# Sixteen-column products ahead of eight blocks left out, eleven warm-up products, and bias rows stored 32 times instead of 128

## The chip, the cores and the metric

The kernel is one launch on one core of a Trainium2 chip. The core has a matrix engine (TensorE, PE in the profile, with its weight loads shown apart as PEld), a vector engine (DVE), a scalar engine (ACT), GpSimd (POOL), a queue engine that issues transfers (SP), and 16 DMA engines which bring data from the chip's memory. Each engine works through its own list of instructions in order and waits on semaphores where it needs something from another. The metric is the device time of the launch in microseconds (us); lower is better.

## What is computed

One decoder layer on 256 tokens of width 2048, everything in float32:

```
h    = rms_norm(x, attn_norm_g);  q, k, v, p = split(h @ w_in)          # 2048 x 4096
q, k = rms_norm per head;         a = softmax(q k^T * scale + bias) v   # 8 heads of 128, causal
m    = (window mean of p over 2/4/8/16 tokens - p) @ pool_w * pool_scale
x    = x + concat(a, m) @ w_out
u    = rms_norm(x, ffn_norm_g) @ w_up                                   # 2048 x 11264
y    = conv_b + causal depthwise convolution (width 3) of u
x    = x + (silu(gate half of y) * value half of y) @ w_down            # 5632 x 2048
```

The bias of a head is a table of 32 learned values, looked up by the distance of query and key; a key after its query gets a very large negative number. With 256 tokens and blocks of 256 the block selection of the reference selects nothing, and plain causal attention is left.

## The kernel before

All weights are laid out on the host in the order of use, as chunks of 128 x 2048 floats (1 MB). A chunk is loaded by SP into one of four `raw` buffers (L111), then split in two: ACT writes `wh`, the weights rounded to the matrix engine's shorter float (L121), and DVE writes `wl`, what the rounding left (L122). The activations are split in the same way into a high and a low part. A product of weights and activations is then three short products: high by high, low by high, high by low; low by low is dropped. Three pairs `wh`, `wl` exist, so PE can be a chunk or so behind the split.

The program is a list `steps` of half chunks, written out by hand. Step `u` uses half `u` of the weights, and after it the functions hooked to that step are issued (`hooks`). Ahead of each even step stands the split of the chunk two further on. The order of the instructions on each engine is the order in which this loop issues them. The stages are:

- 16 steps for the values (`val_half`, L158), 32 steps in token layout for keys and queries (`tok_half`, L168). In between come the sums of squares of the input (L310, L290), the bias row of each head (`bias_rows`, L262) and, from step 35 on, the attention head by head (`scores` L361, `probs_T` L387, `head_out` L397 and L398), placed between the products of the steps.
- 16 steps for the pooling inputs, then 34 for the output projection and the pooling weights. From here on the blocks are in feature layout: `feat_block` makes 256 output features in one accumulator in two halves, from four steps (or three) of eight products each. One such product is a pair of instructions: `wh` against 512 moving columns (high and low part of the activations side by side, L175) and `wl` against 256 moving columns (the high part, L177). This pair is the unit of work of most of the run.
- The feed-forward part: the 22 groups of the inner width go in three thirds (`THIRDS`). A third runs a gate block and a value block for each of its groups, then eight `down` blocks, one for every 256 output features. The very last block uses `feat_sum` (L184), three instructions in place of a pair.

At the first gate block's end `stats2` computes the second norm: `row_scale` multiplies a matrix of ones by the squares in full float32 (L290), which PE does as two passes of 256 columns. These two are issued behind the gate block's last product and ahead of the first value block.

`feat_block` has a flag `lead`. Where it is set, a product of `wh` (128 columns, stationary) and 16 columns of `wl` goes into the accumulator ahead of the block's first product (L490); the first real product then starts that accumulator anew, so nothing of it remains in the result. The flag is set for eight blocks: the third block of the output projection (g == 2), the first gate block of each third, the first value block, and the first down block of each third.

At the very start PE multiplies `ones` by `ones` eight times in full float32 (L218), two passes each, while the first weights are on their way.

The bias: `bias_rows` computes one row of 384 numbers per head (`rsb`, on 8 partitions) and POOL stores it to memory 128 times per head (`band`, L264). `bias_tile` then reads for four heads a tile of 128 x 4 x 256 in which partition p starts one element further left than partition p - 1 (L270), and this shift makes the rows of the distances. The first tile is read at step 24, the second when the fourth head's scores are done. `T`, the tile, shares its buffer with the table `onehot` that `bias_rows` reads.

Of the kernel before, what the change touches and what calls it, by code (L numbers as in the profile page):

```python
# [23 lines left out]
F32 = mybir.dt.float32  # L24
# [5 lines left out]
P = 128  # L30
D = 2048
S = 256
NT = S // P
HD = 128
NH = 8
# [6 lines left out]
L = 384  # L42
CH = 2048
HALF = CH // 2
# [5 lines left out]
OK = (0, 4, 12, 8)  # L50
# [5 lines left out]
def down_order(blocks):  # L56

    a, b, *rest = blocks
    return a[:-1] + b[:-1] + a[-1:] + b[-1:] + [h for c in rest for h in c]
# [18 lines left out]
def layer(ctx: ExitStack, tc: tile.TileContext, xT, wts, par, relT, ident_d, onehot_d, icnt_d, out):  # L78
    nc = tc.nc
# [5 lines left out]
    dram = ctx.enter_context(tc.tile_pool(name="dram", bufs=1, space=bass.MemoryType.DRAM))  # L85
# [3 lines left out]
    def acc(name):  # L89
        return mm.tile([P, 2, 512], F32, name=name, tag="acc")  # L90
# [4 lines left out]
    def small(name):  # L95
        return sm.tile([P, 512], F32, name=name, tag="small")
# [7 lines left out]
    raws, wparts = {}, {}  # L104
# [82 lines left out]
    def feat_half(u, act, k0, ps, first, last, mm=feat_mm):  # L187
        wh, wl = half(u)
        for m in range(2):
            mm(ps[m], wh, wl, act,  # L190
               [(slice(k * 256 + m * P, k * 256 + (m + 1) * P), k0 + k) for k in range(4)],
               first, last)
# [21 lines left out]

    nc.vector.memset(ones, 1.0)
    ps = small("ps_start")
    for _ in range(8):
        nc.tensor.matmul(ps[:, :P], ones, ones, start=True, stop=True)  # L218
    def x_first():
        hi, lo = xh[:, 0, 0, :], xh[:, 0, 1, :]  # L220
# [24 lines left out]
    onehot = early.tile([32, 2 * S], F32, name="onehot", tag="T")  # L245
    rsb = early.tile([NH, L], F32, name="rsb", tag="e", bufs=3)
    icnt = early.tile([P, 4, S], F32, name="icnt")
    band = dram.tile([NH, P, L], F32, name="band")

    def load_consts():  # L250
        nc.sync.dma_start(pv, par)
# [7 lines left out]
    def bias_rows():  # L259
        nc.gpsimd.memset(rsb, NEG)  # L260
        ps = small("ps_rel")
        nc.tensor.matmul(ps[:NH, :S], onehot[:, S:S + NH], onehot[:, :S], start=True, stop=True)  # L262
        nc.vector.tensor_copy(rsb[:, :S], ps[:NH, :S])
        nc.gpsimd.dma_start(band, rsb[:, None, :].to_broadcast([NH, P, L]))  # L264

    def bias_tile(h0):
        t = early.tile([P, 4, S], F32, name="T", tag="T")
        src = bass.AP(tensor=band.tensor, offset=band.offset + h0 * P * L + P - 1,
                      ap=[[L - 1, P], [P * L, 4], [1, S]])
        nc.gpsimd.dma_start(t, src)  # L270
        return t


# [21 lines left out]
    st = {}  # L295
# [149 lines left out]
    def pool_half(u, g0):  # L445

        wh, wl = half(u)
        cat = st["cat"]
        for i in range(2):
            g = g0 - i  # L450
            ps = [(small if i else aux)("ps_pool")[:, :S] for m in range(2)]
            for m in range(2):
                feat_sum(ps[m], wh, wl, cat,
                         [(slice((2 * i + k) * 256 + m * P, (2 * i + k) * 256 + (m + 1) * P), 8 + 2 * g + k)
                          for k in range(2)], True, True)
            st["pool", i] = ps
        for i in range(2):
            g, ps = g0 - i, st.pop(("pool", i))
            parts = [(8 + 2 * g + m, ps[m], col(C_PS + 2 * g + m)) for m in range(2)]
            for k, src, gc in parts:  # L460
                nc.scalar.activation(cat[:, k, 0, :], src, AF.Copy, scale=gc)
            for k, src, gc in parts:
                nc.vector.scalar_tensor_tensor(cat[:, k, 1, :], src, gc, cat[:, k, 0, :].bitcast(F32),
                                               op0=OP.mult, op1=OP.subtract)


    steps, hooks, pre, deferred = [], [], {}, []
# [9 lines left out]
                    post(box["ps"])  # L477
            steps.append([run])

    def feat_block(act, ks, post, final=False, lead=False):  # L480
        box, runs = {}, []
        for i, k0 in enumerate(ks):
            def run(u, i=i, k0=k0):
                if i == 0:
                    box["acc"] = None if final else acc("ps_feat")
                    box["ps"] = [small("ps_feat")[:, :S] if final else box["acc"][:, m, :] for m in range(2)]
                    if lead:
                        wh, wl = wparts[u // 2]
                        o = (u % 2) * HALF
                        nc.tensor.matmul(box["ps"][0][:, :16], wh[:, o:o + P], wl[:, o:o + 16], start=True, stop=True)  # L490
                feat_half(u, act(), k0, box["ps"], i == 0, i == len(ks) - 1, feat_sum if final else feat_mm)
                if i == len(ks) - 1:
                    post(box["ps"] if final else box["acc"])
            runs.append([run])
        return runs
# [5 lines left out]
    XK = (0, 4, 8, 12)  # L501
# [39 lines left out]
    for b in range(2):  # L541
# [4 lines left out]
        for j in range(4):  # L546
            h, u = 4 * b + j, at + 2 * j
# [8 lines left out]
    late = {}  # L556
# [20 lines left out]
    def residual(ps, g):  # L577
        x2 = add_to_x2(ps, g)
        if g == 0:
            nc.scalar.activation(late["sq"], x2, AF.Square)  # L580
            return
        s = late["pool"].tile([P, 2, S], F32, name="xs", tag="y0", bufs=2)
        nc.scalar.activation(s, x2, AF.Square)
        nc.vector.tensor_tensor(late["sq"], late["sq"], s, op=OP.add)

    def x2_split(g):

        if "h" not in late:
            late["h"] = keep.tile([P, KT, 2, S], F32R, name="x2h", tag="h")
        x2, dst = late["x2"], late["h"]  # L590
        for k in range(2 * g, 2 * g + 2):
            nc.scalar.activation(dst[:, k, 0, :], x2[:, k, :], AF.Copy, scale=col(C_FFN + k))
        for k in range(2 * g, 2 * g + 2):
            nc.vector.scalar_tensor_tensor(dst[:, k, 1, :], x2[:, k, :], col(C_FFN + k),
                                           dst[:, k, 0, :].bitcast(F32), op0=OP.mult, op1=OP.subtract)

    def stats2():
        late["rrow"] = keep.tile([P, S], F32, name="rrow2", tag="rrow")
        row_scale(late["rrow"], late["sq"][:, 0, :], late["pool"])

    o0 = len(steps)
    outs = []
    for g in range(D // 256):
        def post(ps, g=g):
            residual(ps, g)
            if g == D // 256 - 1:
                sq = late["sq"]
                nc.vector.tensor_tensor(sq[:, 0, :], sq[:, 0, :], sq[:, 1, :], op=OP.add)
                x2_split(g)
        outs.append(feat_block(lambda: st["cat"], OK, post, lead=(g == 2)))  # L610
    pools = [[lambda u, g=g: pool_half(u, g)] for g in (3, 1)]
    steps += out_order(outs, pools)
    for g in range(D // 256 - 1):
# [25 lines left out]
    def gate(ps, g):  # L639
        if g == 0:  # L640
            stats2()
        conv_in(ps, 0)

        def rest():
            y = conv(2 * g, 0)
            nc.scalar.activation(y, y, AF.Silu)  # L646
            late["gate"] = y
        deferred.append(rest)

    def value(ps, g, j):  # L650
        conv_in(ps, 1)

        def rest():
            if j == 0:
                late["hid"] = keep.tile([P, KT, 2, S], F32R, name="hid", tag="c")
            y = conv(NF + 2 * g, 1)
            hid, ks = late["hid"], slice(2 * j, 2 * j + 2)
            nc.vector.tensor_tensor(y, y, late["gate"], op=OP.mult)  # L658
            nc.scalar.activation(hid[:, ks, 0, :], y, AF.Copy)  # L659
            nc.vector.tensor_tensor(hid[:, ks, 1, :], y, hid[:, ks, 0, :].bitcast(F32), op=OP.subtract)  # L660
        deferred.append(rest)

    def down(ps, g, last, final):
        x2 = late["x2"]
        if final:
            for m in range(2):
                k = 2 * g + m
                nc.vector.tensor_tensor(x2[:, k, :], ps[m], x2[:, k, :], op=OP.add)
                nc.sync.dma_start(out[:, k, :], x2[:, k, :])
            return  # L670
        add_to_x2(ps, g)
        if last:
            nc.sync.dma_start(out[:, 2 * g:2 * g + 2, :], x2[:, 2 * g:2 * g + 2, :])

    for n, (g0, g1) in enumerate(THIRDS):
        for g in range(g0, g1):
            steps += feat_block(lambda: late["h"], XK, lambda ps, g=g: gate(ps, g), lead=(g == g0))
            steps += feat_block(lambda: late["h"], XK, lambda ps, g=g, j=g - g0: value(ps, g, j), lead=(g == 0))
        blocks = []
        for g in range(D // 256):  # L680
            final = n == 2 and g == D // 256 - 1
            blocks.append(feat_block(lambda: late["hid"], range(0, 2 * (g1 - g0), 4),
                                     lambda ps, g=g, n=n, final=final: down(ps, g, n == 2, final), final,
                                     lead=(g == 0)))
        steps += down_order(blocks)

    for u, f in hooks:
# [1 line left out]
    n = len(steps)  # L689
# [76 lines left out]
```

## Time and profile before

| what | value |
|---|---|
| median of 3 runs | 1047.64 us (1046.87 to 1047.82) |
| the profiled execution | 1047.67 us, of which the profile's span is 1045.9 us |
| matrix engine busy | 1039.5 us, 5794 products and 5794 weight loads |
| vector engine, scalar engine busy | 702.7 us, 509.5 us |
| transfers | 200.42 MB, 192 GB/s over the span |

The profile is of one execution. A line such as L175 is the line of the code that issued the instruction, and `ps_feat<-x2h,wh` says which tile it writes and which it reads. "Busy" of PE means that products were under way. Matmuls are pipelined: the next one starts before the one ahead has ended. So the distance from start to start is what one product costs, and its printed duration is longer than that. A product of full float32 is two instructions.

### The profile page before, as it was taken

What the parts mean: (1) busy time and instruction counts of PE and PEld (TensorE: products, weight loads), DVE (VectorE), ACT (ScalarE), POOL (GpSimd) and SP (SyncE); (2) the same over time, 40 slices, a digit from 0 to 9 for tenths busy, and PEclk for the clock granted to TensorE, in tenths of its full rate; (3) what the DMA queues carried; (4) which work ended last, traced back from release to release, by engine and by line L of the source; (5) the groups of instructions that cost most, each with busy time, mean ns of one, the idle gap of its engine ahead of it and who ended that gap; (6) DMA issues with size and microseconds to landing.
All of it is one profiled execution on the core that took longest, in us unless ns stands there. A gap on an engine that the chain in (4) does not pass through costs nothing.

```text
span 1045.9 us, 13805 instructions
## 1 busy us (share of the span) xinstructions
PE 1039.5 (99%) x5794; PEld 897.7 (86%) x5794; DVE 702.7 (67%) x756; ACT 509.5 (49%) x531; POOL 3.7 (0%) x13
## 2 busy tenths in 40 slices
PE   9999999999999999999999999999999999999998
PEld 7887888898888888888888888888888888888887
DVE  6654768967677777776554677777755557777753
ACT  7533555555455545554334454554543445455431
POOL 0000000000000000000000000000000000000000
PEclk9999999999999999999999999999999999999999
DMA  9777554475545555455555555555554545545551
GB/s 349 267 190 225 207 181 162 169 270 182 224 163 201 174 190 200 162 201 201 175 188 187 176 182 194 187 182 184 198 194 169 201 162 201 193 170 189 199 176 41
DMA packets 31534, 200.42 MB, mean 192 GB/s; under 512 B 3832, under 2 KB 4632, under 8 KB 8688
## 3 DMA queue, kind: packets, MB, share of 16 engines
q1 hardware_dynamic: 30480, 196.92, 52.9%
q0 software_dynamic: 992, 2.63, 1.5%
q8 instruction: 45, 0.74, 0.3%
q14 instruction: 17, 0.14, 0.0%
HBM read 195.86 MB, written 3.67 MB: 191 GB/s over the span
## 4 chain that ended last, share of the span: by engine, by line
PE 96%; DMA 3%; DVE 0%; ACT 0%; issue 0%; SPq 0%; ACTq 0%
PE ps_feat L175 55%; PE ps_feat L177 28%; PE ps_tok L168 5%; PE ps_val L158 4%; DMA raw<-in_wts 3%; PE ps_feat L184 1%; PE ps_pool L184 1%; PE ps_s L361 1%; DVE wl L122 0%; ACT wh L121 0%; PE ps_av L397 0%; PE ps_eT L387 0%; PE ps_T L349 0%; PE ps_av L398 0%; PE ps_row L290 0%; PE ps_rel L262 0%
## 5 line engine op out<-in xcount | busy, mean ns | idle before, releaser
L122 DVE TENSOR_TENSOR wl<-raw,wh 128x2048 fp32r<-128x2048 f32 (+2 forms) x187 | 415.6, 2224 | 216.2 <-ACT wh L121 215.8
L175 PE MATMUL ps_feat<-x2h,wh 128*128 128x512 f32 x1408 | 497.6, 397 | 0.0
L121 ACT ACTIVATE wh<-raw 128x2048 fp32r<-128x2048 f32 (+2 forms) x187 | 347.2, 1857 | 117.6 <-PE ps_feat L175 64.2
L177 PE MATMUL ps_feat<-x2h,wl 128*128 128x256 f32 x1408 | 392.8, 279 | 0.0
L175 PEld LDWEIGHTS ps_feat<-x2h,wh 128*128 128x128 f32 x1408 | 263.3, 187 | 67.4
L177 PEld LDWEIGHTS ps_feat<-x2h,wl 128*128 128x128 f32 x1408 | 264.3, 188 | 0.0
L175 PE MATMUL ps_feat<-hid,wh 128*128 128x512 f32 x680 | 240.7, 397 | 0.0
L177 PE MATMUL ps_feat<-hid,wl 128*128 128x256 f32 x680 | 189.8, 279 | 0.0
L175 PEld LDWEIGHTS ps_feat<-hid,wh 128*128 128x128 f32 x680 | 127.2, 187 | 32.5
L413 ACT ACTIVATE fs<-ps_feat 128x512 f32<-128x512 f32 x75 | 45.1, 601 | 181.5 <-PE ps_feat L177 181.5
L177 PEld LDWEIGHTS ps_feat<-hid,wl 128*128 128x128 f32 x680 | 127.6, 188 | 0.0
L414 DVE TENSOR_TENSOR fs<-ps_feat,fs 128x512 f32<-128x512 f32 x75 | 51.7, 689 | 63.8 <-ACT fs L413 63.8
L175 PE MATMUL ps_feat<-cat,wh 128*128 128x512 f32 x256 | 87.5, 390 | 0.0
L168 PE MATMUL ps_tok<-wh,xh 128*128 128x512 f32 x256 | 81.9, 395 | 0.0
L177 PE MATMUL ps_feat<-cat,wl 128*128 128x256 f32 x256 | 70.7, 276 | 0.0
L168 PEld LDWEIGHTS ps_tok<-wh,xh 128*128 128x128 f32 x256 | 48.1, 188 | 10.2 <-issue 0.4
L175 PEld LDWEIGHTS ps_feat<-cat,wh 128*128 128x128 f32 x256 | 48.1, 188 | 10.0
L659 ACT ACTIVATE hid<-y 128x512 fp32r<-128x512 f32 x22 | 13.9, 632 | 86.4 <-DVE y L658 86.4
L168 PE MATMUL ps_tok<-wl,xh 128*128 128x512 f32 x128 | 50.0, 391 | 1.3 <-DVE wl L122 1.3
L177 PEld LDWEIGHTS ps_feat<-cat,wl 128*128 128x128 f32 x256 | 48.1, 188 | 0.0
L632 ACT ACTIVATE y<-u,pv 128x256 f32<-128x256 f32 x88 | 47.6, 591 | 0.9 <-DVE u L623 0.9
L646 ACT ACTIVATE y<-y 128x512 f32<-128x512 f32 x22 | 13.9, 632 | 69.0 <-DVE y L635 69.0
(113 smaller groups left out, 677.9 us busy)
## 6 DMA issues: line engine op xcount, KB each, us to landing
raw<-in_wts SPq DMA_DIRECT2D x177, 1024.0 KB, 4.8
raw<-in_wts SPq DMA_DIRECT2D x6, 512.0 KB, 8.0
xboth<-in_xT SPq DMA_DIRECT2D x7, 256.0 KB, 8.2
out<-x SPq DMA_DIRECT2D x7, 256.0 KB, 2.3
band<-rsb POOLq DMA_DIRECT2D x1, 1536.0 KB, 35.0
raw<-in_wts SPq DMA_DIRECT2D x4, 256.0 KB, 4.6
T<-band POOLq DMA_DIRECT2D x2, 512.0 KB, 6.7
x<-in_xT SPq DMA_DIRECT2D x1, 1024.0 KB, 10.0
```

Of the source, the lines that this page charges most:

```text
L121: nc.scalar.activation(wh, w, AF.Copy)
L122: nc.vector.tensor_tensor(wl, w, wh.bitcast(F32), op=OP.subtract)
L158: nc.tensor.matmul(ps[b][:, t, :], xh[:, k, a, ts], w[:, ws], start=(k == 0 and n == 0), stop=(k == KT - 1 and n == 2))
L168: nc.tensor.matmul(ps[:, t, :], act[:, k0 + k, a, ts], w[:, ws], start=(first and k == 0 and n == 0), stop=(last and k == 1 and n == 2))
L175: nc.tensor.matmul(ps, wh[:, ws], act[:, k, :, :], start=(first and n == 0), stop=False, skip_group_check=True)
L177: nc.tensor.matmul(ps[:, S:], wl[:, ws], act[:, k, 0, :], start=False, stop=(last and n == len(ks) - 1), skip_group_check=True)
L184: nc.tensor.matmul(ps, w[:, ws], act[:, k, a, :], start=(first and n == 0 and i == 0), stop=(last and n == len(ks) - 1 and i == 2))
L413: nc.scalar.activation(dst, ps[:, :, S:], AF.Copy)
L414: nc.vector.tensor_tensor(dst, ps[:, :, :S], dst, op=OP.add)
L632: nc.scalar.activation(y[:, m, :], u[:, m, 2:], AF.Identity, scale=cw[2], bias=col(C_CB + f))
L646: nc.scalar.activation(y, y, AF.Silu)
L659: nc.scalar.activation(hid[:, ks, 0, :], y, AF.Copy)
```

## The change

Three edits are made together.

First, `lead` is taken out of `feat_block` and of its callers, and with it the eight products of L490:

```diff
-    def feat_block(act, ks, post, final=False, lead=False):
+    def feat_block(act, ks, post, final=False):
...
-                    if lead:
-                        wh, wl = wparts[u // 2]
-                        o = (u % 2) * HALF
-                        nc.tensor.matmul(box["ps"][0][:, :16], wh[:, o:o + P], wl[:, o:o + 16], start=True, stop=True)
...
-        outs.append(feat_block(lambda: st["cat"], OK, post, lead=(g == 2)))
+        outs.append(feat_block(lambda: st["cat"], OK, post))
```

Second, the products of `ones` at the start become eleven:

```diff
-    for _ in range(8):
+    for _ in range(11):
         nc.tensor.matmul(ps[:, :P], ones, ones, start=True, stop=True)
```

Third, each head's bias row is stored 32 times, and a tile is read in four pieces of 32 partitions, each piece with a source that starts 32 elements further left:

```diff
-    band = dram.tile([NH, P, L], F32, name="band")
+    band = dram.tile([NH, 32, L], F32, name="band")
...
-        nc.gpsimd.dma_start(band, rsb[:, None, :].to_broadcast([NH, P, L]))
+        nc.gpsimd.dma_start(band, rsb[:, None, :].to_broadcast([NH, 32, L]))
...
-        src = bass.AP(tensor=band.tensor, offset=band.offset + h0 * P * L + P - 1,
-                      ap=[[L - 1, P], [P * L, 4], [1, S]])
-        nc.gpsimd.dma_start(t, src)
+        for q in range(0, P, 32):
+            src = bass.AP(tensor=band.tensor, offset=band.offset + h0 * 32 * L + P - 1 - q,
+                          ap=[[L - 1, 32], [32 * L, 4], [1, S]])
+            nc.gpsimd.dma_start(t[q:q + 32], src)
```

The 1536 KB written become 384 KB; the bytes read for a tile stay 512 KB, in four transfers of 128 KB in place of one.

More of the change, by code (lines that the diff above doesn't have):

```diff
@@ L676, in layer @@
         for g in range(g0, g1):
-            steps += feat_block(lambda: late["h"], XK, lambda ps, g=g: gate(ps, g), lead=(g == g0))
-            steps += feat_block(lambda: late["h"], XK, lambda ps, g=g, j=g - g0: value(ps, g, j), lead=(g == 0))
+            steps += feat_block(lambda: late["h"], XK, lambda ps, g=g: gate(ps, g))
+            steps += feat_block(lambda: late["h"], XK, lambda ps, g=g, j=g - g0: value(ps, g, j))
         blocks = []
@@ L682, in layer @@
             blocks.append(feat_block(lambda: late["hid"], range(0, 2 * (g1 - g0), 4),
-                                     lambda ps, g=g, n=n, final=final: down(ps, g, n == 2, final), final,
-                                     lead=(g == 0)))
+                                     lambda ps, g=g, n=n, final=final: down(ps, g, n == 2, final), final))
         steps += down_order(blocks)
```

## The prediction, made before the changed kernel ran

> **What bounds the kernel now.** I read the page first: the engines' busy times, then who waited for whom on PE.
>
> ```profile
> span 1045.9 us, 13805 instructions
> PE 1039.5 (99%) x5794; PEld 897.7 (86%) x5794; DVE 702.7 (67%) x756; ACT 509.5 (49%) x531; POOL 3.7 (0%) x13
> ...
> PE ps_tok L168 <- DVE wl L122: 1.3, 1, 1.3
> PE ps_val L158 <- ACT wh L121: 0.7, 1, 0.7
> ```
>
> PE has work under way for 99% of the span, and after its start it waits twice, 0.7 and 1.3 us. So the time is the number of products times the distance from one start to the next, and the question is whether that distance is the same everywhere. The groups of instructions give the counts, the windows on L175 the rate, the timeline of PE and the chain the exact starts.
>
> ```profile
> L175 PE MATMUL ps_feat<-x2h,wh 128*128 128x512 f32 x1408 | 497.6, 397 | 0.0
> L175 PE MATMUL ps_feat<-hid,wh 128*128 128x512 f32 x680 | 240.7, 397 | 0.0
> ...
> 231.00:295.00 64.00, 64.00 (x190) 35.37 (x189) 1.00 0.54 193
> 310.00:470.00 160.00, 160.00 (x454) 84.65 (x454) 1.00 0.52 184
> ...
> 230.36 0.39 PE L175 MATMUL ps_feat<-cat,wh 128*128 128x512 f32 x1
> ...
> 295.33 0.47 PE L175 MATMUL ps_feat<-x2h,wh 128*128 128x512 f32 x1
> ...
> 1034.11 8.50 PE ps_feat L184 x72
> ```
>
> In the windows the first number in brackets counts the 512-column products begun or cut by the window's edges. From 230.36 to 295.33 lie 191 pairs (six blocks of 32, less the first pair) and one lead product of 0.03: 64.94 / 191 = **0.3400 us a pair**. From 310 to 470 it is 160 / 453 = 0.353. The clock column says 1.00 in both windows, the instructions have one form, and transfers (0.54 and 0.52 of their time) are no busier in the second. PE has two paces for the same work. The timeline shows where it changes.
>
> ```profile
> 306.30 0.59 PE L290 MATMUL ps_row<-sq,ones 128*128 128x256 f32 x2
> 306.54 0.36 PE L490 MATMUL ps_feat<-wl,wh 128*128 128x16 f32 x1
> 306.75 0.48 PE L175 MATMUL ps_feat<-x2h,wh 128*128 128x512 f32 x1
> ...
> 307.18 0.40 PE L175 MATMUL ps_feat<-x2h,wh 128*128 128x512 f32 x1
> ...
> 307.54 0.40 PE L175 MATMUL ps_feat<-x2h,wh 128*128 128x512 f32 x1
> ```
>
> It changes at the one place where a lead product stands behind full-float32 products (the second norm's row), and from there on every pair, of the up and of the down projection, takes the slow pace to the end. The 32 pairs of the gate block just ahead use the same tiles and buffers, and belong to the fast stretch.
>
> The same kind of disturbance without a lead product occurs earlier, in the attention: `scores` ends with the same 256-column full-float32 product in two passes, and pairs follow at once.
>
> ```profile
> 163.09 0.82 PE L361 MATMUL ps_s<-kT,qT 128*128 128x128 f32 x4
> ...
> 164.10 0.40 PE L175 MATMUL ps_feat<-xh,wh 128*128 128x512 f32 x1
> ...
> 164.45 0.39 PE L175 MATMUL ps_feat<-xh,wh 128*128 128x512 f32 x1
> ...
> 164.79 0.39 PE L175 MATMUL ps_feat<-xh,wh 128*128 128x512 f32 x1
> ...
> 183.26 0.58 PE L175 MATMUL ps_feat<-xh,wh 128*128 128x512 f32 x1
> ...
> 183.80 0.39 PE L175 MATMUL ps_feat<-xh,wh 128*128 128x512 f32 x1
> 184.14 0.39 PE L175 MATMUL ps_feat<-xh,wh 128*128 128x512 f32 x1
> ```
>
> After 163.56 the first pairs are 0.35 apart, then 0.34; after 183.26 they are 0.34 apart at once. Pairs that follow transposes, attention products or pooling products between 150 and 217 us behave in the same way: fast again within a few pairs. I read the pace as a state of PE's two streams, weight loads and products, that the way into a run of pairs decides; I have no row for its cause.
>
> **The change, part by part.**
>
> *Pace (the lead at 306.54 goes).* From 306.75 to 1034.11 lie 1408 - 32 + 680 = 2056 pairs, and five leads of 0.13 each (below): 727.36 - 0.65 = 726.71 us. At the fast pace 2056 x 0.3400 = 699.0. Difference **27.7 us**, if the way from the norm's row into the pairs ends as after `scores`. The bounds of this term alone are 0 and 27.7; I take 27.7, since the nearest rows, of the same form, end fast. Other engines can follow: between 231 and 295 the loads and splits kept up with the fast pace at 193 GB/s.
>
> *The leads' own cost.*
>
> ```profile
> 229.57 0.39 PE L175 MATMUL ps_feat<-cat,wh 128*128 128x512 f32 x1
> ...
> 229.91 0.17 PE L490 MATMUL ps_feat<-wl,wh 128*128 128x16 f32 x1
> ...
> 476.08 0.40 PE L175 MATMUL ps_feat<-x2h,wh 128*128 128x512 f32 x1
> ...
> 477.98 0.40 PE L175 MATMUL ps_feat<-hid,wh 128*128 128x512 f32 x1
> ```
>
> From 229.57 to 230.36 is 0.79 for two pairs and a lead: 0.79 - 0.68 = 0.11. From 476.08 to 477.98 is 1.90 for five slow pairs and a lead: 0.13. Three of the first kind and five of the second: **1.0 us** (0.9 to 1.1). The waits a lead carried move to the block's own first product; the ordinary block starts carry them now, at an even 0.34.
>
> *The bias rows.* The chain of waits leads to the 1.3 us stall.
>
> ```profile
> 68.39 26.45 DMA raw<-in_wts
> ...
> 97.29 0.61 PE L168 MATMUL ps_tok<-wh,xh 128*128 128x512 f32 x2
> 99.22 0.50 PE L168 MATMUL ps_tok<-wl,xh 128*128 128x512 f32 x1 [1.32 <-DVE wl L122]
> ...
> raw<-in_wts SPq DMA_DIRECT2D x177, 1024.0 KB, 4.8
> ...
> band<-rsb POOLq DMA_DIRECT2D x1, 1536.0 KB, 35.0
> T<-band POOLq DMA_DIRECT2D x2, 512.0 KB, 6.7
> ...
> 134.34 0.75 POOL L270 DMA_DIRECT2D T<-band  x1 [36.73 <-DVE mx L368]
> ```
>
> A chunk that lands in 4.8 us as a rule took 26.45 beside the store of `band`, which took 35.0. Two products begin within 0.45 us of 97.29, so the next was due at 97.75 and came at 99.22: **1.5 us** lost. With a quarter of the bytes the store should take about 35.0 / 4 = 8.8 us, and the chunk issued at 68.39 has some 20 us of room more. I take the whole 1.5; the other end is 0, if the tile's four pieces, now issued right behind the shorter store, hold up the loads as the store did. POOL issues four transfers of about 0.75 in place of one, 2.3 us more for each tile, and nothing but a memset for the late stage is queued behind them. The first tile comes earlier than now. The second is issued from 134.34 and would be in by 134.34 + 3.0 + 6.7 = 144, while the scores that read it start at 163.09. SP's queue is not touched.
>
> *The warm-up products.*
>
> ```profile
> 1.05 3.78 PE L218 MATMUL ps_start<-ones 128*128 128x128 f32 x16 [1.05 <-DVE ones L215]
> 5.51 0.80 PE L158 MATMUL ps_val<-wh,xh 128*128 128x512 f32 x1 [0.68 <-ACT wh L121]
> ...
> 6.83 1.05 PE L158 MATMUL ps_val<-wh,xh 128*128 128x512 f32 x2
> ...
> 8.11 1.05 PE L158 MATMUL ps_val<-wh,xh 128*128 128x512 f32 x2
> ...
> 11.55 1.23 DVE L122 TENSOR_TENSOR wl<-raw,wh 128x1024 fp32r<-128x1024 f32 x1 [1.32 <-ACT wh L121]
> ...
> 13.56 0.39 PE L158 MATMUL ps_val<-wl,xh 128*128 128x512 f32 x1
> ```
>
> At 6.83 three products take 8.11 - 6.83 = 1.28, and the steady 0.68 is reached at about 10 us, some 4.5 us after PE took up work at 5.51. Sixteen instructions take 3.78, so six more take about 1.3 and end near 6.1: the gap ahead of 5.51 closes, the work is unbroken for 5 us by then, and the first product is 0.6 late, the third 0.14. If the start-up pace then ends with the warm-up, the third step is held by its `wl` alone, ready at 11.55 + 1.23 = 12.78 where it is used at 13.56: a gain of **0.8 us**. Bounds: -0.15, if the slow start lasts as long as now, and +1.0. I take 0.8, because 5 us of unbroken work is more than the 4.5 that sufficed.
>
> [...]
>
> *Sum.* 27.7 + 1.0 + 1.5 + 0.8 = 31.0 us. The profiled execution took 1047.67, of which 1045.9 is span, and is level with the median of 1047.64: **1016.7 us**. With each term at its ends but the pace fast (27.7 within 0.4, from a spacing read to 0.2 ns): 1047.7 - 28.1 - 1.1 - 1.6 - 1.0 = 1015.9 and 1047.7 - 27.3 - 0.9 - 0 + 0.15 = 1019.7.
>
> **The rivals.**
>
> *The slow pace stays.* The slow pace may belong to the feed-forward part and not to the lead: all five leads inside it were followed by a return to the slow pace, so it is steady there. Against it: 32 pairs of the first gate block run fast on the same tiles. Then only 3.3 us are gained: **1044.4**. [...]
>
> *The pace falls back part way*, at a later block, say where the first down block starts at 476: of 2056 pairs some 480 would be gained, 6.5 us, and the time is about 1038.
>
> *Slower: the slow pace takes hold early.* If the pace hangs on so little, the altered start could put the pairs at the slow pace from the pooling inputs on, at 150 us. There are 128 + 256 + 32 = 416 pairs up to 306, at 0.0135 each 5.6 us, against 3.3 gained: **1049.9**. It decides from about 400 more slow pairs on; with fewer the kernel is level. Against it: every run of pairs in that stretch comes back to 0.34 after a disturbance of its own, with no lead ahead of it but one.
>
> **How the numbers follow.** Fast to the end 0.80; slow pace stays 0.13; falls back part way 0.03; slow early 0.04. The likeliest is the fast case, 1016.7. Its own bounds with the spread of the runs before (1046.87 to 1047.82) are 1015 to 1020.5, and they hold the 8 in 10; the other cases lie outside. A measurement of this kernel tells about 0.2%, 2.1 us, from no change. Faster: 0.80 + 0.03 + 0.10 of the 0.13 (3.3 us, unless the stall or the start gives nothing) = 0.93. Same: the other 0.03. Slower: 0.04.
>
> **What would show it.** Right: L175 x454 between 310 and 470 becomes about x472; the first pairs behind the second norm's row settle at 0.34; L184 starts near 1003; no wait of PE for `wl` near 97; `band` lands in about 9 us; the start-up spacing ends before 7 us. Wrong: starts 0.353 apart after the norm's row, which costs 27.7 at once; a raw load of 20 us beside the four reads; spacing of 0.425 until 10 us.

## The result, and the profile after

The changed kernel takes **1017.18 us** (median of 4 runs, 1017.14 to 1017.41) against 1047.49 for the kernel before in the same sessions (4 runs, 1046.87 to 1047.82): a ratio of 0.9712, interval 0.9697 to 0.9727. The profiled execution took 1017.20 with a span of 1015.4.

Of the kernel after: the page's first lines; who waited for whom on PE (us in total, times, longest); the windows on L175, in the columns of before; and from the chain the start of the last block's products:

```profile
span 1015.4 us, 13822 instructions
...
PE 1010.1 (99%) x5792; PEld 888.2 (87%) x5792; DVE 701.1 (69%) x756; ACT 512.1 (50%) x531; POOL 6.1 (1%) x19
```

```profile
PE ps_start L218 <- DVE ones L215: 1.1, 1, 1.1
PE ps_val L158 <- DVE wl L122: 1.0, 2, 0.8
```

```profile
231.00:295.00 64.00, 64.00 (x189) 35.31 (x189) 1.00 0.57 204
310.00:470.00 160.00, 160.00 (x471) 88.28 (x472) 1.00 0.55 192
```

```profile
1003.70 8.49 PE ps_feat L184 x72
```

PE is busy for 99% of the span, as before; nothing in that figure tells that it works 3% faster. The windows do: 160 us now hold 471 products of L175 where they held 454, at the same clock, and the wait at the keys' and queries' steps (L168) is gone. The clock is not behind it: the 72 products of the last block (L184) take 8.50 us behind pairs 0.353 apart in the kernel before and 8.49 behind pairs 0.340 apart here. The timeline of PE at the place where the pace used to change:

```profile
304.04 0.59 PE L291 MATMUL ps_row<-sq,ones 128*128 128x256 f32 x2
304.28 0.58 PE L175 MATMUL ps_feat<-x2h,wh 128*128 128x512 f32 x1
...
304.82 0.40 PE L175 MATMUL ps_feat<-x2h,wh 128*128 128x512 f32 x1
...
305.17 0.39 PE L175 MATMUL ps_feat<-x2h,wh 128*128 128x512 f32 x1
...
305.52 0.39 PE L175 MATMUL ps_feat<-x2h,wh 128*128 128x512 f32 x1
```

Start to start, the pairs go 0.54, 0.35, 0.35 and then, as the window tells (160 us for 471), 0.34, which is what followed `scores` before. Where the time went is read from four marks that both traces have:

| mark | before | after | earlier by | what lies since the last mark |
|---|---|---|---|---|
| first norm's row, L290, L291 after | 57.22 | 56.85 | 0.37 | the start: 0.37 |
| first scores, L361, L362 after | 110.92 | 108.89 | 2.03 | the stall beside the store: 1.66 |
| second norm's row | 306.30 | 304.04 | 2.26 | two leads: 0.23 |
| first product of L184 | 1034.11 | 1003.70 | 30.41 | the pace and six leads: 28.15 |

### The profile page after: what moved, and what is told of

Its sections match the earlier page's. It is cut to its first block, busy times and chain, and to the rows that moved or that the text cites. A ratio compares the mean times of both kernels' runs of the same rounds, so it can differ in the third digit from the quotient of the medians.

```text
span 1015.4 us, 13822 instructions
## 1 busy us (share of the span) xinstructions
PE 1010.1 (99%) x5792; PEld 888.2 (87%) x5792; DVE 701.1 (69%) x756; ACT 512.1 (50%) x531; POOL 6.1 (1%) x19
## 4 chain that ended last, share of the span: by engine, by line
PE 98%; DMA 1%; SPq 0%; DVE 0%; ACT 0%; issue 0%
PE ps_feat L175 55%; PE ps_feat L177 28%; PE ps_tok L168 9%; PE ps_val L158 4%; PE ps_feat L184 1%; DMA raw<-in_wts 1%; PE ps_pool L184 1%; PE ps_s L362 1%; PE ps_T L350 0%; PE ps_av L398 0%; PE ps_eT L388 0%; PE ps_av L399 0%; SPq L111 0%; SPq L205 0%; DVE wl L122 0%; ACT wh L121 0%
## 5 line engine op out<-in xcount | busy, mean ns | idle before, releaser
L175 PE MATMUL ps_feat<-x2h,wh 128*128 128x512 f32 x1408 | 479.1, 389 | 0.0
L177 PE MATMUL ps_feat<-x2h,wl 128*128 128x256 f32 x1408 | 388.6, 276 | 0.0
L175 PEld LDWEIGHTS ps_feat<-x2h,wh 128*128 128x128 f32 x1408 | 264.3, 188 | 54.7
L175 PE MATMUL ps_feat<-hid,wh 128*128 128x512 f32 x680 | 231.3, 389 | 0.0
L177 PE MATMUL ps_feat<-hid,wl 128*128 128x256 f32 x680 | 187.7, 276 | 0.0
L175 PEld LDWEIGHTS ps_feat<-hid,wh 128*128 128x128 f32 x680 | 127.6, 188 | 26.5
L175 PE MATMUL ps_feat<-cat,wh 128*128 128x512 f32 x256 | 87.4, 390 | 0.0
L168 PE MATMUL ps_tok<-wh,xh 128*128 128x512 f32 x256 | 81.9, 394 | 0.0
L168 PEld LDWEIGHTS ps_tok<-wh,xh 128*128 128x128 f32 x256 | 48.1, 188 | 10.3 <-issue 0.4
L175 PEld LDWEIGHTS ps_feat<-cat,wh 128*128 128x128 f32 x256 | 48.1, 188 | 9.8
L168 PE MATMUL ps_tok<-wl,xh 128*128 128x512 f32 x128 | 49.9, 390 | 0.0
```

The lines of the kernel that those rows point to most:

```text
L168: nc.tensor.matmul(ps[:, t, :], act[:, k0 + k, a, ts], w[:, ws], start=(first and k == 0 and n == 0), stop=(last and k == 1 and n == 2))
L175: nc.tensor.matmul(ps, wh[:, ws], act[:, k, :, :], start=(first and n == 0), stop=False, skip_group_check=True)
L177: nc.tensor.matmul(ps[:, S:], wl[:, ws], act[:, k, 0, :], start=False, stop=(last and n == len(ks) - 1), skip_group_check=True)
```

## The experiments

All times are medians, and each ratio is to the kernel before, run on the same chip in the same session (1047.32 to 1047.41 there). The changed kernel's 1017.18 is from other sessions, where the kernel before took 1047.49, so a difference of a few tenths between it and a run below is a hint and no more.

### One lead taken out, one lead put in

Theory A is that one product, the lead behind the second norm's row, decides the pace of the 2056 pairs that follow. It is tested from both sides. First comes the kernel before without that lead:

```diff
-            steps += feat_block(lambda: late["h"], XK, lambda ps, g=g, j=g - g0: value(ps, g, j), lead=(g == 0))
+            steps += feat_block(lambda: late["h"], XK, lambda ps, g=g, j=g - g0: value(ps, g, j))
```

> The kernel before, with one of its eight lead products left out, that of the first value block behind the second norm's row; everything else as before. Theory A (the pace is decided by the way into a run of pairs, and this one lead product decides it): pairs 0.340 apart to the end, about 2056 x 0.0134 = 27.5 us less than the kernel before, 1020. The seven other leads stand in fast pairs and cost 0.11 each. Rival B (the leads as a group, or the feed-forward part itself, hold the slow pace): the pace changes at the next lead, at the first down block near 476, or not at all: 1041 or 1047.

The changed kernel with only that lead:

```diff
+                    if lead:
+                        wh, wl = wparts[u // 2]
+                        o = (u % 2) * HALF
+                        nc.tensor.matmul(box["ps"][0][:, :lead], wh[:, o:o + P], wl[:, o:o + lead], start=True, stop=True)
...
+            steps += feat_block(lambda: late["h"], XK, lambda ps, g=g, j=g - g0: value(ps, g, j), lead=16 * (g == 0))
```

> The changed kernel, with one lead product put back, that of the first value block. Theory A: slow pace, 0.3535 from there to the end, 1017.2 + 27.6 = 1044.8. Rival B: within 1 us of the changed kernel. Rival C (the start-up or the bias rows had a part in the pace): in between.

Measured: 1019.69 us without it (ratio 0.9737, 0.9723 to 0.9752), 1044.48 with it (0.9973, 0.9963 to 0.9983). The windows on L175 from 310 to 470, of the one and then of the other:

```profile
310.00:470.00 160.00, 160.00 (x471) 88.23 (x471) 1.00 0.55 191
```

```profile
310.00:470.00 160.00, 160.00 (x454) 84.71 (x453) 1.00 0.54 187
```

One product of 16 columns, taken from the kernel before, gives 27.7 us; put into the changed kernel, it costs 27.3. The seven other leads, the start and the bias rows have no part in the pace: with seven leads left it is fast to the end, and with all other edits in place one lead makes it slow. Rivals B and C fall.

### The norm's row computed once more

Is the slow pace a state, or does it belong to the feed-forward part? The same kernel with the one lead, and the row product a second time ahead of the first down block, about 170 us later:

```diff
+                    if row:
+                        nc.tensor.matmul(small("ps_again")[:, :S], ones, late["sq"][:, 0, :], start=True, stop=True)
...
+                                     row=(n == 0 and g == 0)))
```

> As the run with the one lead put back, and ahead of the first down block of the first third the row product of the second norm (ones against the squares, full float32, 256 columns in two passes) is computed once more, into a buffer that nothing reads. Theory A (a state, which a disturbance of the right form sets anew): slow from 304 to about 474, some 480 pairs x 0.0134 = 6.4 us, then fast: about 1024. Rival D (the slow pace belongs to the feed-forward part once it has begun there): slow to the end, 1045.

Measured: 1023.94 (0.9776, 0.9762 to 0.9791). The timeline of PE at the added product, and the windows on both sides:

```profile
473.74 0.40 PE L175 MATMUL ps_feat<-x2h,wh 128*128 128x512 f32 x1
...
474.09 0.59 PE L489 MATMUL ps_again<-sq,ones 128*128 128x256 f32 x2
474.33 0.58 PE L175 MATMUL ps_feat<-hid,wh 128*128 128x512 f32 x1
...
474.87 0.40 PE L175 MATMUL ps_feat<-hid,wh 128*128 128x512 f32 x1
...
475.23 0.39 PE L175 MATMUL ps_feat<-hid,wh 128*128 128x512 f32 x1
...
475.57 0.39 PE L175 MATMUL ps_feat<-hid,wh 128*128 128x512 f32 x1
...
475.91 0.39 PE L175 MATMUL ps_feat<-hid,wh 128*128 128x512 f32 x1
```

```profile
310.00:470.00 160.00, 160.00 (x454) 84.71 (x453) 1.00 0.54 186
480.00:565.00 85.00, 85.00 (x252) 46.93 (x251) 1.00 0.57 198
```

A product that nobody needs, 0.45 us of PE's time, takes the pairs from 0.353 back to 0.34, and they stay there. So the pace is a state: it is set by a disturbance and then lasts. Rival D falls with it, since the same blocks run at both paces.

### Which product does it

Three forms of the lead in the changed kernel at that place: 256 columns, two of 16 columns, and 512 columns (`lead=256`, a loop of two, `lead=512`).

> As the run with the one lead put back, but the lead has 256 columns in place of 16. If a short product behind the full-float32 row makes the slow pace: fast, 1017.2 + 0.1 to 0.2. If any product of this pair of tiles in that place does: slow, about 1045.

> The changed kernel with two 16-column products ahead of the first value block in place of none (before: one). If any product of wh by wl between the norm's row and the pairs makes the slow pace: 1045. If it hangs on an odd number of weight loads there: fast, about 1017.4.

> The changed kernel with one lead ahead of the first value block, of 512 columns, as many as the first product of a pair. If what counts is that a product shorter than a pair's first stands behind the norm's row: fast, 1017.2 + 0.2. If any product of wh by wl there makes the slow pace: 1045.

Measured: 256 columns 1044.54 (0.9974, 0.9963 to 0.9984); two of 16 columns 1044.67 (0.9975, 0.9965 to 0.9984); 512 columns 1017.21 (0.9712, 0.9697 to 0.9726). The timelines of PE, first of the lead with 256, then with 512 columns:

```profile
304.13 0.47 PE L491 MATMUL ps_feat<-wl,wh 128*128 128x256 f32 x1
304.44 0.40 PE L175 MATMUL ps_feat<-x2h,wh 128*128 128x512 f32 x1
...
305.14 0.40 PE L175 MATMUL ps_feat<-x2h,wh 128*128 128x512 f32 x1
```

```profile
304.05 0.58 PE L491 MATMUL ps_feat<-wl,wh 128*128 128x512 f32 x1
304.46 0.40 PE L175 MATMUL ps_feat<-x2h,wh 128*128 128x512 f32 x1
...
305.87 0.39 PE L175 MATMUL ps_feat<-x2h,wh 128*128 128x512 f32 x1
```

The windows on L175 from 310 to 470, of two of 16 columns and then of 512:

```profile
310.00:470.00 160.00, 160.00 (x454) 84.65 (x454) 1.00 0.54 186
```

```profile
310.00:470.00 160.00, 160.00 (x471) 88.26 (x472) 1.00 0.56 192
```

Right behind the lead the two timelines look alike; with 512 columns the pairs are 0.340 apart only from 306.2 on, after five of about 0.35.

The first case of the first expectation, that only a short product does it, was wrong: 256 columns are as bad as 16. Nor is it the number of weight loads, odd or even, as the two leads show. Neither is it the lead as such, for with 512 columns the kernel is level with the changed one. And a lead by itself, behind plain pairs, leaves the pace as it was: 0.340 in the run without the one lead (at 469.73), 0.353 in the kernel before (at 476.43). What separates the five cases is the length of the product that comes right behind the full-float32 row: 512 columns (a pair's own first product, or a lead as long) and the pairs end fast; 16, twice 16 or 256 and they end slow. Lengths in between were not run.

### The same behind the scores

If this is a matter of PE and not of the stage, a short product behind the full-float32 scores must do it too, where the pooling inputs run:

```diff
+        if h >= 4:
+            wh, wl = wparts[(st["q", 1, "end"] + 5 + 2 * j) // 2]
+            nc.tensor.matmul(ps[:, L:L + 16], wh[:, :P], wl[:, :16], start=True, stop=True, skip_group_check=True)
```

> The changed kernel with a 16-column product of wh by wl behind the scores of the last four heads, among the pooling inputs, into columns that nothing reads. If such a product behind a full-float32 one makes the slow pace at any stage: 0.353 from there to the next attention product, about 16 pairs each, 4 x (16 x 0.0134 + 0.11) = 1.3 us, 1018.5. If it does so only in the feed-forward part: 0.34 a pair, and 1017.6 for the four products themselves.

Measured: 1018.08 (0.9720, 0.9706 to 0.9735), 0.9 more than the changed kernel where 1.3 was expected. The timeline of PE behind the first and the fourth of the four:

```profile
161.23 0.36 PE L366 MATMUL ps_s<-wl,wh 128*128 128x16 f32 x1
...
162.23 0.40 PE L175 MATMUL ps_feat<-xh,wh 128*128 128x512 f32 x1
...
162.59 0.40 PE L175 MATMUL ps_feat<-xh,wh 128*128 128x512 f32 x1
...
162.94 0.40 PE L175 MATMUL ps_feat<-xh,wh 128*128 128x512 f32 x1
...
181.79 0.36 PE L366 MATMUL ps_s<-wl,wh 128*128 128x16 f32 x1
182.00 0.47 PE L175 MATMUL ps_feat<-xh,wh 128*128 128x512 f32 x1
...
182.43 0.39 PE L175 MATMUL ps_feat<-xh,wh 128*128 128x512 f32 x1
...
182.77 0.39 PE L175 MATMUL ps_feat<-xh,wh 128*128 128x512 f32 x1
```

Behind the first the pairs stay at 0.35, with no step down to 0.34; so it was behind the second and third, until the next attention product. Behind the fourth they are 0.34 apart at once. So the short product does it in other stages as well, three times out of four. What made the fourth different is open. It alone stands behind products of probabilities and values (L401, L402, from 180.34) as well, and in the kernel before, too, this was the place where the pairs were 0.34 apart at once (183.26). So what ran ahead of the full-float32 product may count beside the length of the next one; no run here tests that.

### Other places in memory

Each buffer of `wh` and `wl` is used from an offset. The changed kernel with other offsets for the chunks from the pooling inputs on:

```diff
-WOFF = ((32, 32), (16, 36))
+WOFF = ((32, 32), (32, 32))
```

> The changed kernel with wh and wl of the later chunks at offsets of 32 and 32 floats in their buffers in place of 16 and 36. If the pace is a matter of how the two streams, weight loads and moving columns, meet in the memory on the chip: another spacing than 0.340 from the pooling inputs on; each 1 ns a pair is 2.5 us. If the pace depends on the order of instructions alone: 0.340 and 1017.2.

Measured: 1035.70 (0.9889, 0.9873 to 0.9906). The windows on L175:

```profile
231.00:295.00 64.00, 64.00 (x183) 34.04 (x182) 1.00 0.52 185
320.00:470.00 150.00, 150.00 (x434) 80.94 (x433) 1.00 0.54 190
```

Less the one or two products that the edges cut, a pair takes about 0.353 in the first window and 0.347 in the second: neither is the 0.340 of the changed kernel, and the norm's row between the windows changes the pace here too. In the first window the pairs start 0.35, 0.35 and 0.36 apart, over and over, where the slow pairs of the kernel before keep to 0.353: the means agree, the rhythms do not. With the instructions as they were, another place of the weights in memory gave other paces: 18.5 us hang on an offset of a few floats (1035.70 for 1017.18). The records of the weight loads themselves last 187 ns on average in both windows (34.04 us for 182, 80.94 for 433), as they do at 0.340 (88.28 for 472), so the pace does not show in them. Whether weight loads and moving columns meet in the memory, which the expectation asks, no run here shows.

### The bias rows

The changed kernel with the rows stored 128 times and read at once, as before; and with 128 copies but the four reads:

```diff
-    band = dram.tile([NH, 32, L], F32, name="band")
+    band = dram.tile([NH, P, L], F32, name="band")
```

> The changed kernel with the bias rows as before: stored 128 times, a tile read at once. Theory (the long store delays a chunk): the wait for wl near 97 returns, 1.5 us and the 0.4 by which PE is now earlier there, 1017.2 + 1.9 = 1019.1. Rival (the stall is taken up later by slack): 1017.2.

> The changed kernel with the rows stored 128 times but read in four pieces. If the store alone makes the stall: as the run with one read, 1019.1. If the tile's single read has a part in it: less, down to 1017.2.

Measured: 1019.01 (0.9730, 0.9716 to 0.9743) and 1018.66 (0.9727, 0.9714 to 0.9740). The timeline of PE in the first, then waits and transfers (from 55 to 105 us) of the second:

```profile
96.36 0.61 PE L168 MATMUL ps_tok<-wh,xh 128*128 128x512 f32 x2
98.28 0.50 PE L168 MATMUL ps_tok<-wl,xh 128*128 128x512 f32 x1 [1.30 <-DVE wl L122]
```

```profile
PE ps_tok L168 <- DVE wl L122: 1.2, 1, 1.2
```

```profile
raw<-in_wts SPq DMA_DIRECT2D x8, 1024.0 KB, 16.7
band<-rsb POOLq DMA_DIRECT2D x1, 1536.0 KB, 35.1
T<-band POOLq DMA_DIRECT2D x4, 128.0 KB, 9.0
```

The wait returns with the long store in both, 1.3 and 1.2 us, and costs 1.8 and 1.5. From the first norm's row to the first scores it is 53.71 and 53.63 us in these two, 53.71 in the kernel before and 52.05 in the changed kernel. Of the changed kernel, the transfers from 55 to 105 us:

```profile
raw<-in_wts SPq DMA_DIRECT2D x9, 1024.0 KB, 4.8
...
band<-rsb POOLq DMA_DIRECT2D x1, 384.0 KB, 9.5
```

The store takes 9.5 us there, and the median load is back at 4.8. The store is the cause; four reads in place of one are level within the spread of these runs (1018.3 to 1019.2).

### The warm-up products

The changed kernel with eight in place of eleven (`range(8)`):

> The changed kernel with eight warm-up products in place of eleven. In the two profiles PE reaches the first norm's row at 57.22 (before) and 56.85 (changed), 0.37 earlier; if that is the warm-up's whole worth: 1017.2 + 0.4 = 1017.6. By the prediction's term, 0.8: 1018.0. If the earlier end of the start-up spacing is given back at the third step's wl: 1017.2.

Measured: 1017.55 (0.9716, 0.9702 to 0.9729), its runs at 1016.75, 1017.13, 1017.96 and 1018.37, where the changed kernel's lie within 0.27. The timeline of PE in the profiled one:

```profile
1.05 3.63 PE L218 MATMUL ps_start<-ones 128*128 128x128 f32 x16 [1.05 <-DVE ones L215]
5.50 0.50 PE L158 MATMUL ps_val<-wh,xh 128*128 128x512 f32 x1 [0.81 <-ACT wh L121]
...
6.56 0.62 PE L158 MATMUL ps_val<-wh,xh 128*128 128x512 f32 x2
...
7.25 0.62 PE L158 MATMUL ps_val<-wh,xh 128*128 128x512 f32 x2
```

In this execution eight products sufficed: from 6.56 on three products take 0.69, where the kernel before, with the same eight, took 1.28 until 10 us. So the end of the slow start is not a matter of the number alone; it falls differently from one execution to the next.

The number seems to count as well, as far as the thirteen profiles of all the runs tell. The spacing of PE is 0.23 by 7 us in all ten with eleven products. Of the three with eight it is so in this one alone; in the kernel before and in the kernel without the one lead it comes down at about 10 and 9.5 us. The first norm's row starts between 56.26 and 56.85 with eleven, at 57.22 and 57.00 behind the two long slow starts, and at 56.39 here. So the long slow starts cost about 0.6 (57.22 and 57.00 against 56.5, the middle of the ten), and eleven products have not shown one. The medians differ by 0.37, less than these runs can tell. Nor is it shown that the spread gets narrower: it is 1.62 with eight and 0.27 with eleven, four runs each, but up to 0.96 in the other kernels with eleven.

## Why the prediction was right

The forecast was 1016.7 us; measured 1017.18. By its own terms, with the gains in us:

| term | predicted | measured | by |
|---|---|---|---|
| pace | 27.7 | 27.4 | 28.15 less six leads (0.11 + 5 x 0.13); with that one lead's own cost 27.7 and 27.3 in two runs |
| leads' own cost | 1.0 | 1.0 | 0.23 for the two in the fast stretch; 0.66 for five at 0.353 a pair (second norm's row to L184: 727.81 before, 727.15 with the one lead alone) |
| bias rows | 1.5 | 1.66 | marks at 57 and 111; the store put back costs 1.8 |
| warm-up | 0.8 | 0.37 | mark at 57 in two executions; eight put back costs 0.4, within their spread |
| sum | 31.0 | 30.5 | 1047.67 - 1017.20 |

*Pace.* The step that carried the forecast was the comparison of the way in: the norm's row with a lead went slow, the scores with the same full-float32 product and no lead went fast. Taking out and putting in that one lead shows it. The prediction had no cause for the pace, and said so: it went by likeness alone, and with a product of 256 columns at that place the likeness would have failed. What the prediction left open, whether a lead as such or its shortness matters, is settled as far as 256 against 512 columns. The rival that kept the slow pace in the feed-forward part rested on the five later leads, which all came back to it; they follow float32 products that had been split, not a full-float32 row, and did not set the state anew. The row computed again did. One product of 16 columns changed the distance of some 2056 pairs behind it, 0.353 for 0.340 with the same columns and at the same clock of 1.00.

*Bias rows.* The store took 9.5 us where 8.8 was worked out, and the whole stall went. It was a little dearer than read (1.66 for 1.5), and part of that is that the two products right behind this wait started wider apart as well (0.34 where 0.23 is the steady step, 99.22 to 99.56 in the kernel before).

*Warm-up.* The third step was indeed held by its `wl`, as forecast; the size was not right:

```profile
1.05 4.72 PE L218 MATMUL ps_start<-ones 128*128 128x128 f32 x22 [1.05 <-DVE ones L215]
5.59 0.49 PE L158 MATMUL ps_val<-wh,xh 128*128 128x512 f32 x1
...
11.44 0.82 PE L158 MATMUL ps_val<-wh,xh 128*128 128x512 f32 x2
13.02 0.50 PE L158 MATMUL ps_val<-wl,xh 128*128 128x512 f32 x1 [0.76 <-DVE wl L122]
13.36 0.64 PE L158 MATMUL ps_val<-wh,xh 128*128 128x512 f32 x2
```

These rows are PE's timeline of the kernel after. The eleven products ended at 5.77, not at 6.1, so the first product was 0.08 late where 0.6 was worked out. The product now at 13.02 stood at 13.56 before, and 12.78 was forecast: its chunk came 0.2 later in this execution, and after the wait the next product starts 0.34 behind it where 0.23 is the steady step. So the wait that took the place of the slow start cost 0.11 here besides its idle time of 0.76. That 5 us of unbroken work end the slow start was the author's estimate from one execution, and as a condition no run shows it: with eight products, in the run above, the spacing was 0.23 from 6.56 on, about 1 us after PE took up work at 5.50 behind an idle 0.81. The term also took one execution for all. It counts a long slow start, which did not come in every profile with eight products; and the profiled execution after is the latest of the ten with eleven at the first norm's row (56.85, their middle 56.5).

## What to carry to other kernels

- When an engine is busy for 99% of the span, compare its distance from start to start between stages that run the same instruction; two values at one clock (0.353 and 0.340 us at 1.00) were 27 us to be had here, and neither the busy share (99% both times) nor the durations (397 and 389 ns) show it plainly.
- When the pace changes, look at the instruction just ahead of the change and at another place with the same neighbours: a test is one product out, or one in. Right behind the norm's full-float32 row a product of 512 columns kept the pace here (1017.21 us), and one of 16 or 256 lost 2.7% (1044.48 and 1044.54).
- A long transfer for a small side task can delay the main stream: beside a store of 35.1 us the median load took 14.8 and 16.7 us in two runs, beside one of 9.5 us it took 4.8. Cutting its bytes to a quarter took the whole delay away here (1.66 us); issuing it at another time was not tried.

## What was not expected of the hardware

- PE has several lasting paces for the same pairs at the same clock (0.340 and 0.353 us with one pair of offsets, about 0.353 and 0.347 with another), and a disturbance chooses among them. A full-float32 product of 0.45 us that nothing reads took it from the worse to the better, worth 20.5 us (1044.48 to 1023.94).
- The choice depends on the length of the one product behind the disturbance: 512 columns good; 16, twice 16 and 256 bad, behind the norm's row. Behind the scores 16 columns were bad three times in four, so the length is not the whole condition.
- Why these paces exist is open. They moved with the place of the weights in memory in the one run with other offsets (1035.70 us for 1017.18); that weight loads and moving columns meet there is a guess which no run shows. A pair of offsets with a pace better than 0.340 was not looked for.
